# Key, query and u projections by seven products for eight, and a fixed TensorE order for the prompt attention

## The chip, the cores and the metric

The kernel runs on one core of one Trainium2 chip. The metric is the device time of one execution in microseconds. TensorE (PE) multiplies; VectorE (DVE), ScalarE (ACT) and GpSimd (POOL) do the elementwise work; SyncE (SP), ACT and POOL issue the transfers. TensorE's clock has two levels, 1.2 and 2.4 GHz; the profile gives the granted clock as a share of the upper one.

## The reference, cut to what matters

One layer of a streaming encoder for 1024 prompt tokens and 8 running streams of 16 new tokens, 1152 rows of width 1024 in all, in float32:

```python
xn = rmsnorm(x)
t = project_tokens(xn)        # gates 3x1024, u, v 512 each, fox q, k, v 512 each, mLSTM q, k, v, o, small columns
y_sg  = u * (W_s layernorm(gelu(v)) + b)          # 128-row chunks; u = gelu(.)
y_fox = softmax(q k^T / 8 + F_q - F_k, causal) v  # 8 heads x 64; prompt 1024 rows, streams with 1024 cached rows
y_ml  = mlstm(conv(q, k), v, gates)               # 4 heads x 128, chunkwise, with state
x = x + (sigmoid(g0)*(y_sg @ W0) + sigmoid(g1)*(y_fox @ W1) + sigmoid(g2)*(y_ml @ W2)) @ W_out
x = x + swiglu(rmsnorm(x)); y = rmsnorm(x)
```

Keys and values of the new rows are outputs too.

## The kernel before, in words

**Products.** Every large product is made in three passes of float32r: each operand is split in a high and a low part, and `mm3` (L113 to L120) issues high x high, high x low and low x high. A weight chunk is 1024 x 256. `load_w` (L86) loads one and splits it on ACT (L94) and DVE (L95). `proj_fm` makes a chunk feature-major, two halves of 128 columns by three groups of 384 tokens, 24 products each: six pieces, 144 products of 384 columns. `proj_tm` makes it token-major, nine tiles of 24 products of 256 columns.

**Seven products for eight.** `seven` (L513) makes a chunk by the scheme of Strassen and Winograd on halves of the contraction, the weight columns and the tokens: `combine_x` prepares the combinations of the tokens once, `weights` (L441) those of the chunk, and 7 x 2 x 12 = 168 products of 288 columns follow; DVE and ACT join the results (`plus`, L473), and SP writes them to DRAM.

**Order of the work.** The program text is a sequence of stages; a scheduler at compile time orders each engine's instructions by that sequence and by when it expects operands, and may take later work early. `keep_in_program_order` pins an instruction to its place in the text. Each engine then runs its queue in order. Stages, with their start in the trace:

1. 0 us: norm and transposition of x, the values of the attention (`v_proj`), gate scans; the first half of u (`bounce_u(0)`) and nine pieces of filler.
2. 145 us: nine chunks by `seven`: the second half of u, four of the mLSTM q and k, four gate chunks.
3. 346 us: prompt attention, head pair by head pair. Per pair the keys and queries are projected with `proj_fm` (`ev_k`, `ev_q` split them straight out of PSUM into `k1`, `k2`, `q1`, `q2`), then 8 query blocks by 2 heads follow: `scores` (L647 to L650, the causal mask as a bfloat16 product), maximum (L652), exponential (L655), scaling (L658) and `values`, which transposes the weights (L668), copies them out (L670 on DVE, L672 on ACT, half each) and multiplies with v (L683).
4. 605 us: spatial gating and the streams' attention, with cached keys and values loaded by POOL.
5. 816 us: mLSTM, four heads; each projects its v and o with `proj_tm` (`w_vo`) and runs a chain over PE, DVE, ACT and POOL. The tail of a head (`tail`: transposition L989, `ym` L993, write to DRAM) is put off until the next head's projection.
6. 1086 us: branch projections (`pz`), then output projection and feed-forward, untouched here.

**Fillers.** `fillers()` is a generator of pieces that nothing waits for at once: 18 of v and 48 of the gates (`FC` = 8 chunks). `fill(n)` puts n of them into the text: 9 ahead of stage 2, 9 after the attention, 24 in the streams' attention, 4, then 2 per head, 4 and 6 in the mLSTM, and the rest before the branch projections.

**Memory.** Pools are stacked: a stage's tiles lie where those of the closed stage before lay, and each tile waits for those it covers. The four inputs of a branch are loaded to `yl` (L1025, issued by ACT) and split to `yh`, `yl` (L438).

Of the kernel before, what the change touches and what calls it, by code (L numbers as in the profile page):

```python
# [29 lines left out]
FB = 22         # feed-forward blocks  # L30
# [10 lines left out]
def emit_(tc, A, top):  # L41
# [7 lines left out]
    mm = nc.tensor.matmul  # L49
# [22 lines left out]
    V.tensor_copy(identb, ident)  # L72
    ones = const.tile([P, P], F32, name="ones")
# [40 lines left out]
    def mm3(out, whs, wls, xhs, xls, first=True, last=True):  # L114
        """out += w^T x over the listed contraction blocks, in three passes of float32r"""
# [10 lines left out]
    def proj_fm_(w, c0, evac):  # L126
        """feature-major projection of 128 weight columns, group by group of tokens"""
# [13 lines left out]
    def proj_tm_(w, n, evac, hook=lambda t: None):  # L141
        """token-major projection of n weight columns, tile by tile of tokens"""
# [11 lines left out]
    def norm(src, gbc, tmp, parts, pin):  # L154
        """rows of a token tile: RMS norm with gain"""
# [12 lines left out]
    def flip(xg, hT, lT, ps_pool):  # L168
        """transposed, split into hT and lT"""
# [8 lines left out]
    def rms_cols(sqs, n, w, ps_pool, pin=lambda i: i):  # L178
        """1 / rms of n tokens, w to a column, from squares that are yet to be summed"""
# [10 lines left out]
    def rms_row(rs, n, w, tmp, ps_pool, pin=lambda i: i):  # L190
        """the same as a row, on every partition"""
# [13 lines left out]
    qk_d = dram("qk_d", [P, 8, T])  # L205
    g_d = dram("g_d", [3, P, KB, T])
# [4 lines left out]
    def bounce(w, c0, dst, func=AF.Copy, scale=1.0, bias=0.0):  # L211
        """feature-major projection kept in DRAM until it is needed"""
# [11 lines left out]
    def bounce_u(j):  # L224
        w = load_w(A["w_u"][j], (KB, 256))
        for i in range(2):
            yield from bounce(w, P * i, u_d[:, 2 * j + i, :], AF.Gelu)

# [8 lines left out]
    def bounce_gate(c):  # L237
        br, j = divmod(c, 4)
        w = load_w(A["w_g"][br, j], (KB, 256))
        for i in range(2):  # L240
            k = 2 * j + i
            yield from bounce(w, P * i, g_d[br, :, k, :], AF.Tanh, 0.5, bg[:, br, k:k + 1])
# [19 lines left out]
    # ================= phase A: norm of the input, transposed =================  # L262
# [38 lines left out]
    # ================= forget and input gates =================  # L301
# [21 lines left out]
    V.scalar_tensor_tensor(c, u, 1.0, e, ALU.subtract, ALU.subtract)     # (u - 1) - e  # L323
# [23 lines left out]
    # running log forget of the attention, in two exact parts, with both signs  # L347
# [15 lines left out]
    # cached rows: log forget from a key to the end of the cache  # L363
# [15 lines left out]
    # mLSTM: running sums b inside a chunk, stabiliser m, and what follows from them  # L379
# [45 lines left out]
    for _ in bounce_u(0):  # L425
        pass
    fill(9)
# [3 lines left out]
    # ================= projections that only the later phases need, in seven products for eight =================  # L431
    # Strassen and Winograd: quarters of the weights and of the tokens are combined first, the products as they leave.
# [48 lines left out]
    def combine_x(s):  # L481
# [5 lines left out]
        for n in range(0, SG, SG // 2):  # L487
# [22 lines left out]
            V.tensor_tensor(b21, b21, b11, ALU.subtract)         # t4 = b21 - t2  # L510
            keep("t4", b21)

    def seven(src, out):  # L513
# [3 lines left out]
        for a, b in (("a11", "b11"), ("a12", "b21"), ("s2", "t2"), ("s3", "t3"), ("s1", "t1"), ("s4", "b22"), ("a22", "t4")):  # L517
            for s in range(2):
# [29 lines left out]
    seven(A["w_u"][1], seven_to(lambda i: u_d[:, 2 + i], AF.Gelu))  # L548
# [8 lines left out]
    kvx = top.enter_context(ExitStack())  # L557
    kvq = pool(kvx, "kvq")
    kve = top.enter_context(ExitStack())
    kvb = pool(kve, "kvb")  # L560
    vt_ = [kvb.tile([P, NT, 256], F32, name=f"v{i}") for i in range(2)]
    for i in range(2):
        nc.scalar.dma_start(vt_[i], A["o_v"][i])

    # ================= phase B: attention over the prompt, head pair by head pair =================
# [3 lines left out]
    ps_t = pool(bs, "ps_t", 1, PSUM)  # L569
    ps_o = pool(bs, "ps_o", 1, PSUM)  # L570
    cfox = kvs.tile([P, P], BF16, name="cfox")
    G.dma_start(cfox, A["c_fox"])
    # q1 = [q_hi; q_lo], k1 = [k_hi; k_hi], q2 = [q_hi; F rows], k2 = [k_lo; F rows]; halves swapped for odd heads
# [5 lines left out]
    zr = fp.tile([P, TP], F32, tag="pe", name="zr", bufs=2)  # L579
    G.memset(zr, 0.0)  # L580
    on = fp.tile([2, TP], F32R, tag="pe", name="on", bufs=2)
# [7 lines left out]
    qbd = kvq.tile([P, 4, NB, 2 * NS], F32, name="qbd")  # L589
    G.memset(qbd, 0.0)  # L590
    kTn = kvq.tile([P, 4, P], F32, name="kTn")
    vn = kvq.tile([P, 4, P], F32, name="vn")
    wq = wk = None
    for hp in range(4):
        v_, v0 = vt_[hp // 2], P * (hp % 2)
        if hp % 2 == 0:
            wk = load_w(A["w_k"][hp // 2], (KB, 256))
            wq = load_w(A["w_q"][hp // 2], (KB, 256))

        # keys  # L600
        def ev_k(g, ps, hp=hp):
            n = min(GW, TP - g * GW)
# [9 lines left out]
            if g == 2:  # L612
                V.tensor_copy(kTn[:, hp, :], ps[:, n:GW])
# [910 lines left out]
```

## Time and profile before

| | |
|---|---|
| runs | 2123.34 us median of 3 (2115.67 to 2124.09) |
| profiled execution | span 2121.1 us from the first to the last instruction; its own time beyond that is not listed |
| mean granted TensorE clock | 0.985 |
| busy | PE 97%, PEld 93%, DVE 61%, ACT 33%, POOL 23% |
| moved | 297.96 MB, mean 140 GB/s |

Busy time of PE counts pipelined matmuls to their modelled end, so it is read together with counts: products per stretch, or the distance from one start to the next. A group line has the line, engine, operation, names, shape and count, then busy us, mean ns of one, and the idle time of the engine before them with what ended it.

### The profile page before, as it was taken

The numbers are of one execution on the slowest core, as the hardware profiler recorded it, in microseconds if no ns is written. First come the engines' busy times: TensorE is split into PE (matmuls) and PEld (weight loads), VectorE is DVE, ScalarE is ACT, GpSimd is POOL, SyncE is SP. The second block draws the span as 40 slices with busy tenths as digits, with TensorE's granted clock in tenths as the row PEclk, the third lists the DMA queues.
The fourth block names the chain that finished last, engine by engine and source line by source line (L and its number), as shares of the span: only waits on it lengthen the run. The fifth ranks groups of instructions, "written<-read, shape, count | busy, mean of one in ns | idle before, by whom it ended". The sixth has DMA issues, their size and how long they took to land. (4 is left out here: it accounts for less than half of the span.)

```text
span 2121.1 us, 37538 instructions
## 1 busy us (share of the span) xinstructions
PE 2053.6 (97%) x15448; PEld 1965.9 (93%) x15448; DVE 1292.6 (61%) x2210; ACT 707.4 (33%) x1353; POOL 485.9 (23%) x526
## 2 busy tenths in 40 slices
PE   7989999999999999999999999899999999999998
PEld 7989999888888899888999999899999999999998
DVE  5785554766533345663334656887787777855566
ACT  5232233544532223443231233332222222333342
POOL 1130002000012221011002224524554544121143
PEclk9999999999999999899999999999999999999999
DMA  4312324010148874322265534124534444455563
GB/s 164 120 51 97 115 85 162 18 59 19 63 161 298 292 239 125 123 97 72 89 199 177 182 137 149 63 100 143 171 136 163 155 157 141 154 206 205 177 223 134
DMA packets 124779, 297.96 MB, mean 140 GB/s; under 512 B 23128, under 2 KB 67352, under 8 KB 116536
## 3 DMA queue, kind: packets, MB, share of 16 engines
q1 hardware_dynamic: 62768, 164.99, 22.2%
q0 software_dynamic: 24512, 87.07, 11.7%
q10 hardware_dynamic: 37328, 43.51, 6.8%
q8 instruction: 121, 1.98, 0.4%
q14 instruction: 50, 0.41, 0.1%
HBM read 213.14 MB, written 82.55 MB: 139 GB/s over the span
## 5 line engine op out<-in xcount | busy, mean ns | idle before, releaser
L118 PE MATMUL ps_st<-xch,whi 128*128 128x288 f32 x1232 | 364.2, 296 | 5.3 <-DVE c L473 5.3
L119 PE MATMUL ps_st<-xcl,whi 128*128 128x288 f32 x1232 | 365.5, 297 | 1.8 <-DVE xcl L438 1.8
L120 PE MATMUL ps_st<-xch,wlo 128*128 128x288 f32 x1232 | 364.4, 296 | 0.9 <-POOL wlo L438 0.9
L118 PEld LDWEIGHTS ps_st<-xch,whi 128*128 128x128 f32 x1232 | 232.9, 189 | 6.6 <-DVE c L473 6.5
L119 PEld LDWEIGHTS ps_st<-xcl,whi 128*128 128x128 f32 x1232 | 232.8, 189 | 2.1 <-DVE xcl L438 2.0
L120 PEld LDWEIGHTS ps_st<-xch,wlo 128*128 128x128 f32 x1232 | 232.6, 189 | 1.1 <-POOL wlo L438 1.1
L118 PE MATMUL ps_fm<-xh,w_hi 128*128 128x384 f32 x624 | 218.6, 350 | 7.3 <-ACT bt L232 4.2
L120 PE MATMUL ps_fm<-xh,w_lo 128*128 128x384 f32 x624 | 215.9, 346 | 0.0
L119 PE MATMUL ps_fm<-xl,w_hi 128*128 128x384 f32 x624 | 215.7, 346 | 0.0
L438 ACT ACTIVATE whi<-w_raw 128x512 fp32r<-128x512 f32 x186 | 107.5, 623 | 312.0 <-DVE w_raw L458 110.1
L118 PE MATMUL po_f<-hh,w 128*128 128x288 f32 x616 | 183.2, 297 | 0.0
L118 PE MATMUL ps_tm<-w_hi,xh 128*128 128x256 f32 (+1 forms) x576 | 171.2, 297 | 11.1 <-ACT bt L232 7.1
L119 PE MATMUL po_f<-hl,w 128*128 128x288 f32 x616 | 181.7, 295 | 0.0
L120 PE MATMUL po_f<-hh,w 128*128 128x288 f32 x616 | 181.3, 294 | 0.4 <-DVE w L438 0.4
L120 PE MATMUL ps_tm<-w_hi,xl 128*128 128x256 f32 (+1 forms) x576 | 170.7, 296 | 0.1
L119 PE MATMUL ps_tm<-w_lo,xh 128*128 128x256 f32 (+1 forms) x576 | 169.9, 295 | 0.0
L438 DVE TENSOR_TENSOR wlo<-w_raw,whi 128x512 fp32r<-128x512 f32 x180 | 160.8, 922 | 5.1 <-ACT whi L438 3.0
L473 DVE TENSOR_TENSOR c<-ps_st,c 128x288 f32<-128x288 f32 x308 | 130.0, 446 | 14.9 <-PE ps_st L120 13.5
L118 PEld LDWEIGHTS ps_fm<-xh,w_hi 128*128 128x128 f32 x624 | 119.1, 191 | 13.4 <-issue 4.5
L118 PEld LDWEIGHTS ps_tm<-w_hi,xh 128*128 128x128 f32 x576 | 114.6, 199 | 14.3 <-ACT bt L232 7.9
L120 PEld LDWEIGHTS ps_fm<-xh,w_lo 128*128 128x128 f32 x624 | 119.0, 191 | 2.7 <-issue 2.4
L119 PEld LDWEIGHTS ps_fm<-xl,w_hi 128*128 128x128 f32 x624 | 119.2, 191 | 1.7 <-issue 1.2
(424 smaller groups left out, 5078.8 us busy)
## 6 DMA issues: line engine op xcount, KB each, us to landing
w_raw<-w_f SPq DMA_DIRECT2D x22, 1024.0 KB
h_d<-hq POOLq DMA_DIRECT2D x66, 288.0 KB, 2.7
kt<-ck POOLq DMA_DIRECT2D x32, 512.0 KB, 6.7
vt<-cv POOLq DMA_DIRECT2D x32, 512.0 KB, 7.0
hl<-h_d SPq DMA_DIRECT2D x28, 576.0 KB
gt<-g_d ACTq DMA_DIRECT2D x96, 144.0 KB
w_raw<-w_g SPq DMA_DIRECT2D x12, 1024.0 KB
g_d<-bt SPq DMA_DIRECT2D x48, 192.0 KB
```

What stands on the lines that cost most here:

```text
L118: mm(out, lhsT=whs[i], rhs=xhs[i], start=(first and i == 0), stop=False)
L119: mm(out, lhsT=whs[i], rhs=xls[i], start=False, stop=False)
L120: mm(out, lhsT=wls[i], rhs=xhs[i], start=False, stop=(last and i == n - 1))
L438: return act(hi, src, AF.Copy), (eng or V).tensor_tensor(lo, src, f32(hi), ALU.subtract)
L473: V.tensor_tensor(out, ps, other, ALU.add)
```

## The change

- Both chunks each of the keys, queries and u, and one gate chunk more, are made by `seven`. Keys go to the output `o_k`, queries to a new DRAM array `q_d`. Stage 2 has 15 chunks instead of 9.
- Both chunks of v (18 tiles) are made at the end of stage 1, where the first half of u and nine pieces stood. The fillers are only gate pieces, 7 chunks of 6; the first two chunks are written raw, and their tanh is applied when they are read in the branch projections.
- The attention loads a pair's keys, queries and values from DRAM (`head_load`, a pair ahead), splits them in `head_split` on ACT, DVE and POOL, and is issued as 32 steps (pair, query block) in which every TensorE instruction is pinned: scores of one head, values of the block before the last, transposition of the last block's first head, scores of the other head, transposition of the second. Twelve filler pieces stand at fixed places around the change of pairs. The mask is a float32r product; a third of the copies of the transposed weights is on DVE, the rest on ACT.
- The streams' q, k and v are loaded from DRAM at the start of their stage.

```diff
-FC = 8          # gate chunks that fill other phases; the other four go in seven products
+FC = 7
+RC = 2
...
+    def mm(*a, **k):
+        r = nc.tensor.matmul(*a, **k)
+        return tc.keep_in_program_order(r) if pinned[0] else r
...
     def fillers():
-        for j in range(2):
-            yield from bounce_v(j)
+        ws = [gate_w(0)]
         for c in range(FC):
-            yield from bounce_gate(c)
+            if c + 1 < FC:
+                ws.append(gate_w(c + 1))
...
+                if c < RC:
+                    yield from bounce(ws[c], P * i, g_d[br, :, k, :])
+                else:
+                    yield from bounce(ws[c], P * i, g_d[br, :, k, :], AF.Tanh, 0.5, bg[:, br, k:k + 1])
...
     v_proj(1)
-    for _ in bounce_u(0):
-        pass
-    fill(9)
+    for j in range(2):
+        for _ in bounce_v(j):
+            pass
...
-    seven(A["w_u"][1], seven_to(lambda i: u_d[:, 2 + i], AF.Gelu))
+    for j in range(2):
+        seven(A["w_k"][j], seven_to(lambda i, j=j: A["o_k"][2 * j + i]))
+        seven(A["w_q"][j], seven_to(lambda i, j=j: q_d[2 * j + i]))
+    for j in range(2):
+        seven(A["w_u"][j], seven_to(lambda i, j=j: u_d[:, 2 * j + i], AF.Gelu))
...
+    def head_load(hp):
+        raw = []
         for i in range(2):
+            for src in (A["o_k"], q_d):
+                r = fp.tile([P, TP], F32, tag="kq", name="kq", bufs=4)
+                for a in H:
+                    nc.sync.dma_start(r[a], src[hp, H[i], :TP])
+                raw.append(r)
...
+    def head_split(hp, raw):
+        for i in range(2):
+            kk, qq = raw[2 * i:2 * i + 2]
+            a, b = H[i], H[1 - i]
+            act(k1[i], kk, AF.Copy)
+            act(q1[i], qq, AF.Copy, scale=0.125)
+            V.tensor_tensor(k2[i][a, :], kk[a, :], f32(k1[i][a, :]), ALU.subtract)
+            G.tensor_copy(q2[i][a, :], f32(q1[i][a, :]))
+            V.scalar_tensor_tensor(q1[i][b, :], qq[b, :], 0.125, f32(q1[i][b, :]), ALU.mult, ALU.subtract)
...
-                    mm(ps[:, d:n], lhsT=identb, rhs=cfox, start=False, stop=True)
+                mm(ps[:, d:w], lhsT=identr, rhs=cfox, start=False, stop=True)
...
-                if (qi + i) % 2:
+            evacs[0] += 1
+            if evacs[0] % 3 == 0:
                     V.tensor_copy(pt_s[:, j:j + w, :], pt[:, :w, :])
...
+    pinned[0] = True
+    fill(2)
+    for n, st_ in enumerate(steps):
+        hp, qi = st_
+        if qi == 0:
+            if n:
+                values(steps[n - 2])
+                turned(steps[n - 1], 0)
+                fill(1)
+                turned(steps[n - 1], 1)
+                fill(1)
+            scores(st_, 0)
+            scores(st_, 1)
+        else:
+            scores(st_, 0)
+            if qi > 1 or n > 1:
+                values(steps[n - 2]) if n > 1 else None
+            turned(steps[n - 1], 0)
+            scores(st_, 1)
+            if qi == 1:
+                fill(1)
+            turned(steps[n - 1], 1)
+        if qi == 0 and hp < 3:
+            raw, vs[hp + 1] = head_load(hp + 1)
+        if qi == KB - 1 and hp < 3:
+            head_split(hp + 1, raw)
+    values(steps[-2])
+    for i in range(2):
+        turned(steps[-1], i)
+    values(steps[-1])
+    pinned[0] = False
-    fill(9)
...
+                if 4 * br + j // 2 < RC:
+                    act(gt, gt, AF.Tanh, scale=0.5, bias=bg[:, br, j:j + 1])
```

## Rows read from the trace of the kernel before

**Rows 1.** The page, part 1: busy us of each engine (share of the span) xinstructions.
```profile
PE 2053.6 (97%) x15448; PEld 1965.9 (93%) x15448; DVE 1292.6 (61%) x2210; ACT 707.4 (33%) x1353; POOL 485.9 (23%) x526
```
**Rows 2.** Windows of four stretches: length, busy (xcount) of PE, PEld, DVE, ACT, POOL, clock, DMA.
```profile
145.10:345.90 200.80, 200.80 (x1514) 200.80 (x1513) 111.61 (x217) 56.44 (x98) 5.80 (x3) 1.00 0.28 102
...
604.90:632.60 27.70, 23.55 (x149) 21.54 (x148) 6.49 (x9) 4.79 (x8) 6.81 (x13) 0.88 0.79 265
...
841.60:905.40 63.80, 58.49 (x390) 54.41 (x389) 44.20 (x73) 26.15 (x68) 6.97 (x6) 0.87 0.33 104
905.40:957.70 52.30, 49.43 (x374) 45.90 (x373) 31.39 (x59) 22.18 (x65) 6.86 (x5) 1.00 0.30 97
```
**Rows 3.** Windows, PE, tile ps_fm (feature-major pieces) alone: length, busy (xproducts).
```profile
345.90:373.70 27.80, 25.24 (x144) 1.00 0.49 185
...
373.70:604.90 231.20, 89.00 (x434) 1.00 0.11 38
...
604.90:815.70 210.80, 133.04 (x672) 0.97 0.77 264
...
1012.20:1085.70 73.50, 64.52 (x336) 1.00 0.33 112
```
**Rows 4.** The same for tile ps_tm (token-major tiles).
```profile
373.70:604.90 231.20, 18.90 (x113) 1.00 0.11 38
...
815.70:841.60 25.90, 25.90 (x216) 1.00 0.42 120
```
**Rows 5.** Groups by line of PE, 373.7 to 604.9 us: the attention.
```profile
L683 PE MATMUL po<-pT,v 128*64 128x128 f32 x576 | 53.0, 281 | 0.0
...
L668 PE MATMUL pt_p<-ident,pe 128*128 128x128 f32 x288 | 49.7, 281 | 0.9 <-DVE pe L658 0.9
```
**Rows 6.** Timeline of PE in the second head pair: start us, us, instruction, xcount merged.
```profile
464.17 0.60 PE L668 MATMUL pt_p<-ident,pe 128*128 128x128 f32 x4
464.53 0.48 PE L647 MATMUL ps_s<-k,q 128*128 128x512 f32 x1
464.84 0.39 PE L648 MATMUL ps_s<-k,q 128*128 128x512 f32 x1
465.07 0.39 PE L647 MATMUL ps_s<-k,q 128*128 128x512 f32 x1
...
465.85 1.52 PE L683 MATMUL po<-pT,v 128*64 128x128 f32 x22
467.31 0.66 PE L668 MATMUL pt_p<-ident,pe 128*128 128x128 f32 x4
```
**Rows 7.** Groups by line of DVE, all forms together, 373.7 to 604.9 us.
```profile
L652 DVE TENSOR_REDUCE mx<-ps_s 128x1 f32<-128x128 f32 (+7 forms) x64 | 47.8, 751 | 19.1 <-PE ps_s L650 18.7
L658 DVE TENSOR_SCALAR pe<-pe,rc 128x128 f32<-128x128 f32 (+7 forms) x64 | 33.0, 518 | 2.3
L670 DVE COPY pT<-pt_p 128x512 f32<-128x512 f32 (+3 forms) x48 | 26.5, 553 | 13.4 <-PE pt_p L668 13.2
```
**Rows 8.** Timeline of POOL where the attention's tiles are set up.
```profile
348.31 1.04 POOL L585 CAST q<-zr 64x1024 fp32r<-64x1024 f32 x1 [4.49 <-DMA g_d<-c]
...
353.47 1.03 POOL L586 CAST k<-zr 64x1024 fp32r<-64x1024 f32 x1
```
**Rows 9.** Timeline, last mLSTM head to the branch projections: PE's last pn products.
```profile
1029.64 0.65 PE L952 MATMUL pn<-Cs,qx 128*32 128x129 f32 x16
```
**Rows 10.** The same stretch, POOL: the reciprocal root of the head's norm.
```profile
1041.84 1.82 POOL L83 TENSOR_TENSOR r<-r,mhalf 128x9 f32<-128x9 f32 x1
```
**Rows 11.** The same stretch, DVE: the last scaling before the head's transposition.
```profile
1043.70 1.36 DVE L982 TENSOR_TENSOR nd<-nd,r 128x1152 f32<-128x1152 f32 x1 [3.79 <-POOL r L83]
```
**Rows 12.** The same stretch, ACT (ACTq: a transfer that ACT issues).
```profile
1054.61 0.37 ACT L993 ACTIVATE ym<-pt_h,mlg 128x128 f32<-128x128 f32 x1 [0.68 <-DMA yml_d<-ym]
...
1065.20 0.33 ACTq L1025 DMA_DIRECT2D yl<-ysg_d  x1
...
1071.00 1.17 ACT L438 ACTIVATE yh<-yl 128x1152 fp32r<-128x1152 f32 x1 [1.09 <-DMA yl<-ysg_d]
```

More of the change, by code (lines that the diff above doesn't have):

```diff
@@ L72, in emit_ @@
     V.tensor_copy(identb, ident)
+    identr = const.tile([P, P], F32R, name="identr")
+    V.tensor_copy(identr, ident)
     ones = const.tile([P, P], F32, name="ones")
@@ L205, in emit_ @@
     qk_d = dram("qk_d", [P, 8, T])
+    q_d = dram("q_d", [4, P, T])
     g_d = dram("g_d", [3, P, KB, T])
@@ L222, in emit_ @@
     V.tensor_scalar(bg, bg, 0.5, None, ALU.mult)
[L224 to L227, printed above, removed]
     def bounce_v(j):
@@ L555, in emit_ @@
     es.close()
[L557 to L563, printed above, removed]
     bs = top.enter_context(ExitStack())
@@ L568, in emit_ @@
     ps_s = pool(bs, "ps_s", 2, PSUM)
-    ps_t = pool(bs, "ps_t", 1, PSUM)
+    ps_f = pool(bs, "ps_f", 1, PSUM)
     ps_o = pool(bs, "ps_o", 1, PSUM)
-    cfox = kvs.tile([P, P], BF16, name="cfox")
-    G.dma_start(cfox, A["c_fox"])
+    banks[:] = [(ps_f, "f", 1)]
+    cfox = fp.tile([P, P], F32R, name="cfox")
+    cf = fp.tile([P, TP], F32, tag="pe", name="cf", bufs=3)
+    nc.scalar.dma_start(cf[:, :P], A["c_fox"])
+    V.tensor_copy(cfox, cf[:, :P])
     H = (slice(0, 64), slice(64, 128))
@@ L578, in emit_ @@
     k2 = [fp.tile([P, TP], F32R, name=f"k2{i}") for i in range(2)]
-    zr = fp.tile([P, TP], F32, tag="pe", name="zr", bufs=2)
+    zr = fp.tile([P, TP], F32, tag="pe", name="zr", bufs=3)
     G.memset(zr, 0.0)
-    on = fp.tile([2, TP], F32R, tag="pe", name="on", bufs=2)
+    on = fp.tile([2, TP], F32R, tag="pe", name="on", bufs=3)
     G.tensor_scalar(on, zr[:2, :], 1.0, None, ALU.add)
@@ L696, in emit_ @@
-    fill(9)
+    def head_load(hp):
+        raw = []
+        for i in range(2):
+            for src in (A["o_k"], q_d):
[3 more added lines that the diff above has]
+                raw.append(r)
+        v_ = fp.tile([P, KB, P], F32, tag="vh", name="vh", bufs=2)
+        nc.scalar.dma_start(v_, A["o_v"][hp // 2][:, :KB, P * (hp % 2):P * (hp % 2) + P])
+        return raw, v_
@@ new lines, in emit_, with scores @@
+    pes, pTs, pos, vs = {}, {}, {}, {}
+    evacs = [0]
+    def scores(n, i):
+        hp, qi = n
+        w = P * (qi + 1)
+        qs = slice(P * qi, P * qi + P)
+        ps = ps_s.tile([P, TP], F32, tag="s", name="ps_s")
+        for c in range(0, w, 512):
+            e = min(c + 512, max(w, c + 256))
+            d = w - P if w - P < e else None
+            mm(ps[:, c:e], lhsT=q1[i][:, qs], rhs=k1[i][:, c:e], start=True, stop=False)
+            mm(ps[:, c:e], lhsT=q2[i][:, qs], rhs=k2[i][:, c:e], start=False, stop=(d is None))
+            if d is not None:
+                mm(ps[:, d:w], lhsT=identr, rhs=cfox, start=False, stop=True)
+        mx = small.tile([P, 1], F32, tag="mx", name="mx")
+        V.tensor_reduce(mx, ps[:, :w], AX.X, ALU.max, negate=True)
+        pe = fp.tile([P, TP], F32, tag="pe", name="pe", bufs=3)
+        sm_ = small.tile([P, 1], F32, tag="sm_", name="sm_")
+        act(pe[:, :w], ps[:, :w], AF.Exp, bias=mx, accum_out=sm_)
+        rc = small.tile([P, 1], F32, tag="rc", name="rc")
+        V.reciprocal(rc, sm_)
+        V.tensor_scalar(pe[:, :w], pe[:, :w], rc, None, ALU.mult)
+        pes[n, i] = pe
@@ new lines, in turned @@
+    def turned(n, i):
+        pe = pes.pop((n, i))
+        pT = fp.tile([P, KB, P], F32, tag=f"pT{i}", name="pT", bufs=1)
+        for j in range(0, n[1] + 1, 4):
+            w = min(4, n[1] + 1 - j)
+            pt = ps_mm.tile([P, 4, P], F32, tag="mm", name="pt_p", bufs=2)
+            for x_ in range(w):
+                flipped(pt[:, x_, :], pe[:, (j + x_) * P:(j + x_ + 1) * P], ident)
+            evacs[0] += 1
+            if evacs[0] % 3 == 0:
+                V.tensor_copy(pT[:, j:j + w, :], pt[:, :w, :])
+            else:
+                act(pT[:, j:j + w, :], pt[:, :w, :], AF.Copy)
+        pTs[n, i] = pT
@@ new lines, in values @@
+    def values(n):
+        hp, qi = n
+        qg, qo = divmod(qi, 4)
+        if qo == 0:
+            pos[0] = ps_o.tile([P, 512], F32, tag="o", name="po")
+        po = pos[0]
+        o = slice(P * qo, P * qo + P)
+        for j in range(qi + 1):
+            for x_ in range(2):
+                mm(po[H[x_], o], lhsT=vs[hp][:, j, 64 * x_:64 * x_ + 64], rhs=pTs[n, x_][:, j, :],
+                   start=(j == 0), stop=(j == qi))
+        if qo == 3:
+            yf = fp.tile([P, 512], F32, tag="yf", name="yf", bufs=1)
+            act(yf, po, AF.Copy)
+            nc.sync.dma_start(yfox_d[:, hp, 512 * qg:512 * qg + 512], yf)
@@ new lines, in emit_ @@
+    steps = [(hp, qi) for hp in range(4) for qi in range(KB)]
+    raw, vs[0] = head_load(0)
+    head_split(0, raw)
+    pinned[0] = True
[11 more added lines that the diff above has]
+            scores(st_, 1)
+        else:
+            scores(st_, 0)
[10 more added lines that the diff above has]
+            head_split(hp + 1, raw)
@@ L697, in emit_ @@
+    values(steps[-2])
+    for i in range(2):
+        turned(steps[-1], i)
+    values(steps[-1])
+    pinned[0] = False
     bs.close()
-    kve.close()
+    banks[:] = [(ps_mm, "mm", 2)]
     ds = top.enter_context(ExitStack())
     sp = pool(ds, "smp")
+    kTn = sp.tile([P, 4, P], F32, name="kTn")
+    nc.scalar.dma_start(kTn, A["o_k"][:, :, TP:].rearrange("h p t -> p h t"))
+    vn = sp.tile([P, 4, P], F32, name="vn")
+    for i in range(2):
+        nc.scalar.dma_start(vn[:, 2 * i:2 * i + 2, :], A["o_v"][i][:, 8, :].rearrange("p (h d) -> p h d", d=P))
@@ L703, in emit_ @@
+    qbd = sp.tile([P, 4, NB, 2 * NS], F32, name="qbd")
+    G.memset(qbd, 0.0)
+    qs_ = sp.tile([P, 4, NB, NS], F32, tag="v", name="qs_", bufs=2)
+    nc.scalar.dma_start(qs_, q_d[:, :, TP:].rearrange("h p (b q) -> p h b q", q=NS))
+    for hp in range(4):
+        for i in range(2):
+            act(qbd[H[i], hp, :, NS * i:NS * i + NS], qs_[H[i], hp], AF.Copy, scale=0.125)
     ps_s = pool(ds, "ps_s3", 1, PSUM)
@@ L838, in emit_ @@
     banks.pop()
-    kvx.close()
     fill(4)
```

109 lines of the change are left out of this document (10 added, 99 removed).

## The prediction

> **What bounds the kernel now.** I read the page's first part, then windows by stage, then groups and the timeline inside the stages that change. The first part says TensorE: 97% busy, the next engine at 61% [rows 1]. That share is of modelled ends, so I go by paces. In the seven-product stage 1514 products pass in 200.8 us, 0.133 us each at full clock, and nothing waits [rows 2]; the feature-major pieces of 384 columns run at 25.24 / 144 = 0.175 us, the token-major ones of 256 columns at 25.9 / 216 = 0.120 us [rows 3, 4]. Nearly all of the span is such dense work. So time changes in two ways only: TensorE's work gets smaller, or a place opens where its queue has nothing to do. The reader should look in the rows for how much of the cover behind slow chains consists of filler, since the change spends it elsewhere.
>
> **The change part by part.**
>
> *Seven products for eight.* A full chunk is 144 products, 25.2 us; by seven it is 168 x 0.133 = 22.3 us. Six chunks change over (four of keys and queries, one of u, one gate): 6 x 2.9 = 17.5 us less. DVE, which joins the results, is busy 111.6 of 200.8 us there [rows 2], so it stays hidden at the same density; with no cover a chunk would cost DVE's 12 us. In stage 1 nine token-major tiles (25.9 us) replace six pieces of u (25.2): +0.7.
>
> *The attention's own work.* From 345.9 to 604.9 us are 259.0 us. Out of them go 576 products of keys and queries (100.8 us) and 113 of v (13.6) [rows 3, 4]: 144.6 us are left, 36.2 per head pair. What must be in a pair: by the code 24 score products of 512 columns, 16 of 256 and 8 of 384, at 0.23 (464.84 to 465.07), 0.12 and 0.175: 8.8 us; 288 / 4 = 72 transpositions at 0.36 for four: 6.5; 576 / 4 = 144 value products at 1.46 for 22: 9.6 [rows 5, 6]. That is 24.9. The other 11.3 us are changes between kinds of product (the first score product behind transpositions takes 0.31 instead of 0.23 [rows 6]), table loads and waits.
>
> After the change a step has five groups, hence five changes. The values' own is in their pace; four at 0.08 for eight steps are 2.6 us. The 16 mask products become float32r of 128 columns, which no row shows; between nothing and the 0.23 of a 512-column one I take the 0.12 of 256 columns: 1.9. The pinned order makes every product wait behind the one ahead of it: a transposition that waits for DVE's scaling holds the next scores, and with them the next maximum. DVE's work per pair is (47.8 + 33.0 + 2/3 of 26.5) / 4 = 24.6 us [rows 7] and an estimated 2.5 of reciprocals, 27, against TensorE's 29.4. So near a balance queues will not mesh fully; I take 2.5 us of waits (0 to 7, where 7 is what remains of the 11.3). A pair: 31.9.
>
> At the start the tiles that hold the F rows wait until the last results of the seven-product stage are written: POOL begins at 348.3, and its four casts end at 354.5 [rows 8]. POOL's copies of q and SP's row transfers come behind them, an estimated 5 us, so scores start at about 359.5; the two pinned filler pieces (8.4 us) end at 354.3. A hole of 5 us. At the end the last block's chain has nothing beside it: 3 us. Sum 4 x 31.9 + 5 + 3 = 135.6 against 144.6: 9 us less (19 less with no waits, 16 more with 7 us of waits and masks at 0.23). At a change of pair the new split (some 5 us each on ACT and DVE, 2 on POOL) and its SP transfers lie behind two filler pieces, two transpositions and a group of values, about 11 us; uncovered it would be 3 us a pair.
>
> The Trainium skill, *TensorEngine Tiling (Array Packing)*, Key Properties, says that a change of tiling mode drains the engine. Values use half the columns (128*64), so each of their groups would drain twice; the trace holds it in the 1.46 us for 22 of them, the change included, and cannot part it from the products. By that rule fewer and longer groups alone bring the 19 us of the case without waits, the second rival below.
>
> *Streams' attention.* Behind the attention now lie 103 leftover products of v, 12.4 us, while the first keys are loaded; even so that stretch has 23.6 of 27.7 us busy at clock 0.88 [rows 2, 4]. They go; 30 filler pieces remain where 672 / 24 = 28 are used now [rows 3], so some move forward: +4 us (0 to 12). The new loads of q, k, v and eight ACT copies are issued beside the cached keys' transfers.
>
> *mLSTM.* Of 42 pieces 12 go into the attention and 28 into the streams: 2 are left for four heads, against 20 now. Moving them costs nothing; the holes they leave do. Inside a head the next head's v and o tiles can move up, but their gate tile has one buffer, so only four tiles (11.5 us) fit before the head's norm is done. What a head costs when the chain shows: the first takes 63.8 us at clock 0.87, the second 52.3 at 1.00, with 390 and 374 products [rows 2]. Two heads lose 8.4 us of filler each; between 0 and 11.5 each I take 5: +10.
>
> The last head has no next one. Now 336 filler products, 58.8 us, lie from its start to the branch projections [rows 3]. Its last pn products end at 1030.3 [rows 9]; POOL's root ends at 1043.7 [rows 10], the scaling at 1045.1 [rows 11]. Of these 14.8 us TensorE has 3 of its own: a hole of 12. Before that, in the 18 us from the head's first product, another 4. Then `ym` is copied and written by about 1057; the branch inputs lie where this head's tiles were, and the third one's load takes 5.8 us to its split [rows 12]; with the earlier start I take 8. Together +24 (10 if the inputs' space is free early, 35 if all loads queue behind the tail).
>
> The Trainium skill, *TensorE: Matmul & The Clock Gate*, HAM oscillation, warns that gaps between bursts of matmuls bring the clock back to 1.2 GHz. The 0.87 above, a mean of the two levels, agrees. By it the branch products behind the hole would start at half rate, an estimated 3 us on top.
>
> The tanh of two gate chunks on ACT, 16 operations, lies beside branch products; ACT is the idler engine there.
>
> *Sum.* -17.5 + 0.7 - 9 + 4 + 10 + 24 = +12. The profiled span is 2121.1 us; the median of the runs is 2.2 above. Forecast 2121.1 + 12 + 2.2 = 2135 us, 0.6% slower.
>
> **Rivals.**
>
> *The holes don't open* (faster). The scheduler moves the next head's tiles and the branch products up into the last heads. For it: the first branch needs nothing of this head. Against: its inputs' place in memory. Of 34 us of holes some 6 remain: 2107. It decides from the point where they stay under 11 us, since all other terms add up to -22.
>
> *The pinned order runs free of waits.* TensorE's 29.4 exceeds DVE's 27; against it, the chain of maximum, exponential and scaling has one step to finish. 10 us less: 2125.
>
> *DVE sets the attention's pace.* In the wide blocks its work is about TensorE's, and a pinned queue cannot step aside. +25: 2160.
>
> **How the numbers follow.** Forecast 0.45 (own range 2120 to 2152), holes stay shut 0.27, no waits 0.18, DVE 0.10. A measurement of this kernel tells 0.5%, 11 us, from no change. Faster: 0.25 of the first rival, 0.04 of the second, 0.29. The same: 0.02, 0.14 and 0.08 of the forecast's low end, 0.24. Slower: 0.37 and 0.10, 0.47. The range goes from below the first rival to beyond the third: 2095 to 2166.
>
> **What would show it.** Seven products: 15 chunks at 22.3 us, 2520 products without a gap. Attention: 186 us with 288 filler products in it; TensorE's waits name DVE's scaling or ACT's copies. mLSTM: no feature-major product behind the first head, and waits of the transposition of the last head and of the first branch products of some 20 us, with a clock under 1. It is wrong if the branch products start within 8 us of the last head's pn products, or if the attention needs more than 200 us.

## The result and the profile after

The changed kernel takes 2184.94 us (median, 2174.86 to 2188.74) against 2123.72 for the kernel before on the same chip: ratio 1.0296, 95% interval 1.0264 to 1.0329, slower. The profiled execution spans 2179.3 us against 2121.1. The forecast was 2135: its direction came true, its size is 50 us short and its range (2095 to 2166) does not hold the result. First the engines' shares on the page, which answer to [rows 1]:

```profile
PE 2040.0 (94%) x15592; PEld 1966.2 (90%) x15592; DVE 1322.9 (61%) x2252; ACT 715.1 (33%) x1377; POOL 496.7 (23%) x533
```

TensorE is busy 13.6 us less and the span is 58.2 longer. The windows by stage say where. Their columns are those of [rows 2]; in order: seven products, start of the attention, the rest of it, streams, the four mLSTM heads, the branch products.

```profile
149.00:483.80 334.80, 334.80 (x2522) 334.80 (x2521) 188.50 (x367) 90.60 (x160) 4.78 (x3) 1.00 0.28 101
483.80:506.50 22.70, 8.79 (x50) 8.15 (x48) 5.43 (x5) 5.67 (x6) 4.31 (x4) 0.78 0.87 245
506.50:686.50 180.00, 167.57 (x1360) 146.81 (x1360) 124.74 (x241) 104.28 (x226) 14.26 (x11) 0.97 0.27 77
686.50:914.20 227.70, 214.87 (x1973) 189.84 (x1971) 84.68 (x140) 54.42 (x103) 52.51 (x98) 0.99 0.75 254
914.20:955.30 41.10, 35.59 (x254) 32.68 (x253) 31.01 (x56) 14.19 (x23) 9.35 (x4) 0.96 0.39 119
955.30:1003.50 48.20, 41.49 (x318) 39.86 (x318) 33.52 (x55) 21.82 (x63) 7.58 (x6) 0.89 0.27 76
1003.50:1065.90 62.40, 53.24 (x351) 47.54 (x350) 31.13 (x67) 16.01 (x60) 2.10 (x2) 0.81 0.18 65
1065.90:1132.20 66.30, 39.81 (x246) 34.11 (x245) 23.26 (x46) 23.71 (x82) 4.15 (x4) 0.73 0.30 97
1132.20:1292.90 160.70, 158.14 (x1152) 155.93 (x1153) 88.71 (x175) 40.90 (x65) 28.25 (x32) 0.97 0.55 168
```

The clock column is the quickest guide: 1.00 in the seven products, 0.78 in the start of the attention, then a fall from head to head, 0.96, 0.89, 0.81, 0.73. A stage's length alone misleads, because filler was moved between stages. So the table takes each stage without it (a feature-major product at 0.175 us, a token-major one at 0.120), and from each head also its other products at the pace that they have in the last head of the kernel before, where the clock is 1.00 and nothing waits:

| step of the forecast | forecast, us | measured, us |
|---|---|---|
| six chunks by seven products | -17.5 | -17.3 (334.8 / 15 = 22.32 a chunk; six of them less 864 x 0.175) |
| stage 1 | +0.7 | +3 (TensorE waits 8.4 for the gelu copies of v, 6.4 before) |
| attention's own work | -9 | +8 (202.7 - 50.4 = 152.3 against 144.6) |
| streams | +4 | +3 |
| mLSTM heads 1 to 3 | +10 | +13 (-7, +6, +14) |
| last head, start of the branch products | +24 | +44 (36 and 8) |
| the rest | 0 | +4 |
| sum | +12 | +58 |

Where the heads' time goes is seen in TensorE's waits from 914 to 1140 us (what it waited for, us in total, times, longest):

```profile
PE pt_h L1021 <- DVE nd L1014: 10.2, 1, 10.2
PE ps_tm L53 <- ACT to L937: 8.3, 3, 4.7
PE ps_st L53 <- DVE wt L965: 7.6, 5, 3.0
PE pu L53 <- DVE Cc L974: 6.2, 5, 3.8
PE pz L53 <- ACT yh L450: 6.2, 2, 5.6
```

These are links of the heads' own chain, which filler covered before. In all TensorE is idle for 47.9 us in the four heads, 8.8 before. The last head in the timeline (start, duration, engine, instruction), answering to [rows 9 to 12]:

```profile
1107.00 0.65 PE L53 MATMUL pn<-Cs,qx 128*32 128x129 f32 x16
...
1119.05 1.83 POOL L95 TENSOR_TENSOR r<-r,mhalf 128x9 f32<-128x9 f32 x1
1120.91 1.36 DVE L1014 TENSOR_TENSOR nd<-nd,r 128x1152 f32<-128x1152 f32 x1 [5.13 <-POOL r L95]
1122.33 1.12 PE L1021 MATMUL pt_h<-ident,nd 128*128 128x128 f32 x4 [10.22 <-DVE nd L1014]
...
1126.63 0.33 ACTq L1057 DMA_DIRECT2D yl<-ysg_d  x1
1131.26 0.33 ACTq L1057 DMA_DIRECT2D yl<-ysg_d  x1
1132.20 1.33 PE L53 MATMUL pz<-yh,w_hi 128*128 128x288 f32 x4 [5.61 <-ACT yh L450]
1134.00 0.44 PE L53 MATMUL pz<-yh,w_lo 128*128 128x288 f32 x1
1134.24 0.44 PE L53 MATMUL pz<-yl,w_hi 128*128 128x288 f32 x1
```

From the last pn product to the transposition TensorE has almost nothing to do; the branch inputs are asked for only behind the last copy, at 1126.6; and the first branch products follow at 0.24 us, not at 0.133: the lower clock level. The same trace holds one thing more. The inputs of the second branch, which have other space, are asked for between 1087.0 and 1104.8 and are split by 1112.6, 20 us before the first branch product; but TensorE's queue has the first branch next. Whether the second branch, taken first, would fill this hole was not tried.

### The profile page after: what moved, and what is told of

Its sections match the earlier page's. It is cut to its first block, busy times and chain, and to the rows that moved or that the text cites. A ratio compares the mean times of both kernels' runs of the same rounds, so it can differ in the third digit from the quotient of the medians.

```text
span 2179.3 us, 38038 instructions
## 1 busy us (share of the span) xinstructions
PE 2040.0 (94%) x15592; PEld 1966.2 (90%) x15592; DVE 1322.9 (61%) x2252; ACT 715.1 (33%) x1377; POOL 496.7 (23%) x533
## 3 DMA queue, kind: packets, MB, share of 16 engines
q1 hardware_dynamic: 65328, 175.74, 23.4%
## 5 line engine op out<-in xcount | busy, mean ns | idle before, releaser
L450 ACT ACTIVATE whi<-w_raw 128x512 fp32r<-128x512 f32 x222 | 128.6, 623 | 398.6 <-PE ps_x L53 173.2
L53 PE MATMUL po_f<-hh,w 128*128 128x288 f32 x1232 | 248.6, 296 | 0.7 <-DVE w L450 0.7
L53 PEld LDWEIGHTS po_f<-hh,w 128*128 128x128 f32 x1232 | 198.2, 188 | 1.3 <-DVE w L450 1.1
L450 DVE TENSOR_TENSOR wlo<-w_raw,whi 128x512 fp32r<-128x512 f32 x216 | 174.5, 839 | 11.0 <-ACT whi L450 7.4
L485 DVE TENSOR_TENSOR c<-ps_x,c 128x288 f32<-128x288 f32 x210 | 92.8, 454 | 129.2 <-PE ps_x L53 110.7
L53 PE MATMUL pz<-yh,w_hi 128*128 128x288 f32 x384 | 113.0, 300 | 7.4 <-ACT yh L450 7.2
L53 PE MATMUL ps_fm<-xh,w_hi 128*128 128x384 f32 x336 | 118.8, 353 | 0.6 <-ACT bt L228 0.6
L53 PEld LDWEIGHTS ps_tm<-w_hi,xl 128*128 128x128 f32 x576 | 116.2, 202 | 1.1 <-issue 0.4
L53 PEld LDWEIGHTS ps_tm<-w_lo,xh 128*128 128x128 f32 x576 | 116.1, 202 | 0.6
L53 PE MATMUL ps_fm<-xh,w_lo 128*128 128x384 f32 x336 | 115.8, 345 | 0.0
```

The lines of the kernel that those rows point to most:

```text
L53: r = nc.tensor.matmul(*a, **k)
L485: V.tensor_tensor(out, ps, other, ALU.add)
```

## The experiments

Medians are of the runs of each kernel; ratios against the kernel before, with 95% intervals.

**Is it the filler?** Ten gate chunks as filler in the changed kernel (the weights of the later ones are loaded when they start):

```diff
-FC = 7
+FC = 10
...
```

> The changed kernel with ten gate chunks as filler instead of seven (two by seven products instead of five), so that 20 pieces are left for the four mLSTM heads and the tail instead of 2. Theory A (what the heads and the tail lost was their filler, and with it the clock): three chunks cost 3 x 2.9 = 8.7 us more on TensorE, and the 57.6 us lost between the first mLSTM product and the end of the branch projections come back almost whole: 2185 + 9 - 58 = 2136, with 244 us from the first score product of the mLSTM to the first branch product as before, and a granted clock of at least 0.95 there instead of 0.83. Rival B (the holes come from the head's own chain and its loads, the filler only shifts them): the 18 pieces add up to their own 75 us less what fits in 48 us of idle time, so 2185 + 9 + 0 to 27, about 2195 to 2220.

Measured 2129.63 us, ratio 1.0030 (1.0014 to 1.0046). The third and fourth head and the branch products:

```profile
...
965.00:1016.60 51.60, 50.95 (x382) 46.54 (x381) 20.10 (x45) 16.40 (x60) 6.65 (x3) 1.00 0.21 74
1016.60:1090.10 73.50, 73.50 (x455) 69.41 (x454) 27.02 (x46) 23.91 (x52) 2.08 (x2) 1.00 0.34 112
1090.10:1242.70 152.60, 152.60 (x1153) 152.60 (x1152) 89.42 (x176) 44.41 (x68) 27.12 (x32) 1.00 0.61 190
```

The last head with 336 filler products is 7.2 us longer than the one without any (66.3, which holds 120 token-major products instead), and nothing waits in it. Three chunks made as filler cost TensorE 3 x 2.88 = 8.6 us more than by seven products, so in all 2179.3 + 8.6 - 2127.2 = 60.7 us of span came back. The reverse, in the kernel before:

```diff
-FC = 8
+FC = 5
```

> The kernel before with five gate chunks as filler instead of eight (seven by seven products instead of four): nothing of the change but its lack of filler, 2 pieces for the mLSTM and the tail instead of 20. Theory A: three chunks by seven products save 8.7 us, and the heads and the tail lose the 57.6 us that they lost in the changed kernel: 2124 - 9 + 58 = 2173, with the transposition of the last head waiting some 10 us and a clock near 0.83. Rival B (the loss needs the rest of the change, such as keys and queries in DRAM or the new loads): 2124 - 9 + 0 to 15, that is 2115 to 2130. The forecast's own price of the holes (34) would give 2149.

Measured 2174.90, ratio 1.0237 (1.0213 to 1.0262). Last head and branch products:

```profile
1061.00:1127.60 66.60, 39.83 (x247) 34.15 (x246) 23.30 (x46) 23.66 (x81) 4.15 (x4) 0.73 0.29 96
1127.60:1288.50 160.90, 159.36 (x1153) 157.05 (x1154) 88.51 (x175) 33.84 (x49) 27.22 (x32) 0.96 0.55 168
```

The same 66 and 161 us, without anything else of the change. Its span is 2173.2, and 2121.1 - 8.6 + 60.7 = 2173.2. Taken away, the pieces give the loss; put back, they end it. This settles what the main loss is: 18 pieces of filler, 76 us of products that the change took out or spent earlier, covered 61 us of waits and slow products.

**Which pieces?** The 18 are parted: 12 pieces, all for the last head and the tail; or 6, two for each of the last three heads. Both edits are shown against the kernel with ten chunks:

```diff
-FC = 10
+FC = 9
-        fill(2)
+        fill(2 if h == 0 else 0)
```

> The changed kernel with nine gate chunks as filler: 12 pieces more, all of them for the last mLSTM head and what follows it, while the three heads between get none (2 pieces in the first, as in the changed kernel). It parts the price of the holes. Reading of the changed kernel's trace: 24.3 us of idle time and 8 us of low clock from the last head on, and 8.1 us in the branch products, 40 us; that is 2185 + 2 x 2.9 - 40 = 2151. By the forecast's own sizes (24 for the tail, 10 for the heads): 2185 + 6 - 24 = 2167. If the holes between the heads weigh as much as the rest (29 each): 2162.

Measured 2147.30, ratio 1.0115 (1.0081 to 1.0150).

```diff
-FC = 10
+FC = 8
```

> The counterpart: eight gate chunks as filler, 6 pieces more, two for each of the second to fourth heads, and none behind the last head. By the reading of the trace (some 18 us lost between the heads, of them 7 to 13 as idle time and the rest as clock): 2185 + 2.9 - 18 = 2170. By the forecast's 10 us: 2178. Together with the kernel for the tail alone the two gains should add up to the 57.6 us that ten chunks brought back; if they add up to more, each closes part of the same hole; if to less, a hole needs both.

Measured 2146.22, ratio 1.0109 (1.0076 to 1.0142). In spans the tail's pieces brought 2179.3 + 5.8 - 2143.7 = 41 us, the heads' 2179.3 + 2.9 - 2143.9 = 38, together 80, where both at once brought 61. So some 19 us are closed by either, and my 18 for the heads was less than half. The third and fourth head of the second kernel, and its branch products, show how:

```profile
...
1006.90:1058.50 51.60, 50.95 (x383) 46.55 (x382) 20.09 (x45) 16.39 (x60) 6.65 (x3) 1.00 0.18 63
1058.50:1100.30 41.80, 24.56 (x167) 20.21 (x165) 20.79 (x44) 13.71 (x40) 2.08 (x2) 0.77 0.42 135
1100.30:1260.70 160.40, 159.13 (x1153) 156.81 (x1154) 91.42 (x177) 43.14 (x67) 28.24 (x32) 0.96 0.56 172
```

The third head, with 48 filler products more, takes 51.6 us instead of 62.4, its clock 1.00 instead of 0.81. And the last head's token-major tiles (120 products of them lie in the last head of the changed kernel) are done a head earlier. The four heads hold 98, 338, 218 and 2 token-major products here and 98, 217, 218 and 121 in the changed kernel (216 make a head's nine tiles; a count may include two of a neighbour's): with two pieces a head all nine tiles of the next head are made a head ahead, without them only four, and five are left for the head itself. Why the pieces make that difference no run shows.

**Is the low clock a price of its own?** Six pieces in the last head and behind it whose results nobody reads:

```diff
...
+        if h == 3:
+            for _ in range(2):
+                idle_piece()
...
-    fill(4)
+    for _ in range(4):
+        idle_piece()
```

> The changed kernel with 6 pieces of 24 products more in the last mLSTM head and behind it, of the size of a filler piece (25 us of products), whose results nobody reads. They take no work from anywhere else, so whatever they gain is not the filling of the hole but what the hole does to the products around it. In the changed kernel the last head takes 66.3 us with 26.5 us of idle time and the products between them at half rate (granted clock 0.73), and the branch products 160.7 us instead of 152.6. Theory (the low clock is a price of its own, some 12 us in the last head and 8 in the branch products): the pieces cost nothing where TensorE is idle, the rest of the last head runs faster, and the branch products take 152.6: 2185 - 8 - 0 to 8 = 2169 to 2177. Rival (only idle time counts): the pieces that do not fit push the chain back, 2185 to 2195. The forecast named 3 us for the clock: 2182.

Measured 2189.17, ratio 1.0315 (1.0276 to 1.0353): the rival's number. Windows of the last head, the branch products, the chain from the first pu to the last pn product, and the first 104 branch products:

```profile
1071.20:1143.60 72.40, 58.30 (x391) 53.51 (x390) 21.31 (x44) 21.53 (x80) 4.16 (x4) 0.90 0.22 73
1143.60:1305.80 162.20, 157.64 (x1152) 155.44 (x1153) 91.23 (x177) 42.96 (x67) 28.33 (x32) 0.98 0.56 174
1094.00:1107.70 13.70, 13.70 (x103) 12.29 (x104) 8.35 (x22) 2.23 (x8) 0.00 (x0) 1.00 0.12 39
1143.60:1167.00 23.40, 18.84 (x105) 16.64 (x106) 11.29 (x14) 11.89 (x19) 0.00 (x0) 0.86 0.62 193
```

and the same two short stretches of the changed kernel:

```profile
1088.70:1107.40 18.70, 12.71 (x69) 9.98 (x67) 11.82 (x25) 5.50 (x11) 0.00 (x0) 0.73 0.44 140
1132.20:1154.10 21.90, 19.34 (x105) 17.13 (x106) 8.78 (x12) 10.22 (x18) 0.00 (x0) 0.78 0.52 156
```

The chain took 13.7 us at clock 1.00 instead of 18.7 at 0.73, although 37 products were put into it. At most these 5 us go with the clock, for the clock is not the only difference. In the changed kernel DVE splits three of the second branch's inputs inside the chain (busy 11.82 us against 8.35), and a step of the chain stands behind the last of these splits:

```profile
1104.46 1.36 DVE L450 TENSOR_TENSOR yl<-yl,yh 128x1152 fp32r<-128x1152 f32 x1 [0.69 <-ACT yh L450]
...
1106.14 0.49 PE L53 MATMUL pn<-va,wt 128*128 128x129 f32 x2 [1.41 <-DVE nd L987]
```

With the unread products these splits come only behind the chain, from 1135.7 on, so some 1.4 of the 5 us are theirs. The forecast's 3 us for the clock, given there beside the Trainium skill's *TensorE: Matmul & The Clock Gate*, HAM oscillation, were for another place, the branch products. The gain did not last: most of the other unread products ran as one block from 1114.9 to 1130.2 ahead of the transposition, which came 22.5 us behind the last pn product instead of 14.9. Then two loads of the second branch went out ahead of the first branch's (1130.3 and 1134.5 before 1138.2), so that the first branch products began 10.6 us behind the last transposition instead of 6.1. And they ran no faster, 104 of them in 23.4 us with clock 0.86 against 21.9 with 0.78. So the clock alone does not explain their 8 us.

**What holds the first branch products?** The four loads of their inputs, 4 us apart on ACT's queue, were the next suspect:

```diff
-            nc.scalar.dma_start(f32(lo), yd[:, k, :])
+            (nc.scalar if n else nc.sync).dma_start(f32(lo), yd[:, k, :])
```

> The changed kernel with the four loads of the first branch's inputs issued on SP's queue instead of ACT's. In the changed kernel they are issued at 1126.6, 1131.3, 1135.3 and 1139.1 us, 4 us apart, each behind ACT's splitting of the one before. Theory (this row of loads holds the first branch products): on SP they go out one behind the other within 2 us, the first 104 products take some 15 us instead of 21.9, and the time falls by 6 to 8: 2177 to 2179. Rival (the low clock holds them, 0.78 in this stretch): at most 2 us, 2183 to 2185.

Measured 2185.57, ratio 1.0297 (1.0273 to 1.0321).

```profile
1133.96 6.22 SPq L1057 DMA_DIRECT2D yl<-ysg_d  x4
1140.19 1.15 ACT L450 ACTIVATE yh<-yl 128x1152 fp32r<-128x1152 f32 x1
```

The four went out over 6 us, not within 2, and the first was ready only at 1140.2. The first branch product came 8.9 us behind the last transposition instead of 6.1, and the first 104 took 18.9 us instead of 21.9: 27.8 us from the last transposition to the 104th, before this edit 28.0, with clock 0.91 and 0.78. The edit moved the wait and did not shorten it; neither the queue nor the clock alone holds this stretch. The same edit where nine chunks are filler (below):

> The kernel with nine gate chunks as filler, a free attention order and a bf16 mask, with the same four loads on SP's queue. With nine chunks the first 104 branch products took 24.3 us instead of 13.8. By the theory of the loads most of that comes back: 2125 - 8 = 2117, level with ten chunks. By the rival: 2123 to 2125.

Measured 2125.30, ratio 1.0009 (0.9992 to 1.0027), against 2124.81 without it: no gain either. What is left is the time of the transfers (four of 576 KB, among gate tiles of 144 KB each); that was not tried.

**The start of the attention.** In the changed kernel the scores begin 22.7 us after the seven products with 8.4 us of cover. SP's queue, then the instructions that follow:

```profile
488.62 0.33 SPq L105 DMA_DIRECT2D w_raw<-w_g  x1
...
493.72 0.32 SPq L229 DMA_DIRECT2D g_d<-bt  x1
494.30 0.57 SPq L598 DMA_DIRECT2D q<-on  x1
...
496.50 2.11 SPq L608 DMA_DIRECT2D kq<-o_k  x2
501.74 1.06 ACT L618 ACTIVATE k<-kq 128x1024 fp32r<-128x1024 f32 x1 [8.04 <-DMA kq<-o_k]
505.23 1.22 DVE L622 SCALAR_TENSOR_TENSOR q<-kq,q 64x1024 fp32r<-64x1024 f32 x1 [1.19 <-ACT q L619]
506.51 0.58 PE L53 MATMUL ps_s<-k,q 128*128 128x256 f32 x1 [13.34 <-DVE q L622]
```

The first pair's loads moved ahead of the constant rows:

```diff
+    raw, vs[0] = head_load(0)
     zr = fp.tile([P, TP], F32, tag="pe", name="zr", bufs=3)
...
-    raw, vs[0] = head_load(0)
     head_split(0, raw)
```

> The changed kernel with the first head pair's loads of keys and queries issued ahead of the preparation of the constant rows (zeros, ones), which in the changed kernel stand ahead of them on SP's queue and reach 496.5 us. Theory C (the order on SP's queue makes the hole): the loads are issued about 7 us earlier, at 489, and the scores begin 7 us earlier: 2178. Rival D (the space of the loaded tiles comes free only with the last writes of the seven-product stage, and the constant rows are then late instead): no more than 2 us, 2183 to 2185.

Measured 2188.32, ratio 1.0296 (1.0270 to 1.0322); scores 22.3 us after the seven products.

```profile
489.27 1.33 SPq L597 DMA_DIRECT2D kq<-o_k  x2
493.58 0.33 SPq L229 DMA_DIRECT2D g_d<-bt  x1
494.01 1.09 SPq L597 DMA_DIRECT2D kq<-q_d  x2
498.51 1.06 ACT L607 ACTIVATE k<-kq 128x1024 fp32r<-128x1024 f32 x1 [4.96 <-DMA kq<-o_k]
```

Asked for 7 us earlier, the keys were there 3 us earlier: 9.2 us under way instead of 5.2. And the queries' load stands behind the second filler piece's write, which waits for that piece. Then the values' load out of the way as well; the next gate chunk's weights were to come later too, but their transfer was issued at 488.7 as before, so only the values tell:

```diff
...
-        nc.scalar.dma_start(v_, A["o_v"][hp // 2][:, :KB, P * (hp % 2):P * (hp % 2) + P])
+        (nc.scalar if hp else nc.sync).dma_start(v_, A["o_v"][hp // 2][:, :KB, P * (hp % 2):P * (hp % 2) + P])
...
     head_split(0, raw)
+    vs[0] = load_v(0)
```

> The kernel with the early loads of the first head pair, and besides the values' load of this pair (1 MB) issued behind them on SP's queue and the next gate chunk's weights (1 MB) loaded three pieces later. With the early loads alone the first keys were asked for 7 us earlier, but took 9 us to land instead of 5, all DMA engines being busy at 0.99 from 488 us on. Theory (the transfers' place in the traffic makes the hole): the first keys and queries land 4 to 5 us after 489.5 and the scores begin near 500 instead of 506: 2188 - 6 = 2182, against 2185 for the changed kernel 2179 to 2182. Rival (POOL's copies and the constant rows, which wait for the last writes of the stage before, come last): scores at 504 or later, 2185 to 2188.

Measured 2178.02, ratio 1.0265 (1.0226 to 1.0303). The keys came at 497.0, 7.4 us after the issue, and the scores begin 18.2 us after the seven products, at 502.1:

```profile
502.11 0.58 PE L53 MATMUL ps_s<-k,q 128*128 128x256 f32 x1 [8.87 <-DVE q L616]
```

The scores gained 4.5 of the 6 us that were expected. With the values' 1 MB off ACT's queue the keys were 7.4 us under way instead of 9.2. This fits the Trainium skill, *DMA: Bandwidth & Descriptors*, Queues, rings and completion order, by which a DMA engine takes turns between the queues that have work for it. One profile of each kernel does not show that this is the reason.

**The fixed order.**

```diff
-    pinned[0] = True
+    pinned[0] = False
```

> The changed kernel with the same attention, but its products not kept in the order of the program. By the forecast's step (a pinned queue waits where a free one steps aside, and its two filler pieces at the start end before the scores can begin) the filler pieces move forward into the hole at the start: 14 us and some clock less there, about 2168. But the pieces that move are then missing at the changes of head pair: if those need them, up to 3 us a pair return, 2168 to 2177. Rival (the fixed order itself is a gain, since the free one has more changes between kinds of product, 36.2 us a pair as before instead of 34): 2168 + 8 = 2176 or more, no better than 2185 if the pairs also lose their cover.

Measured 2171.83, ratio 1.0230 (1.0200 to 1.0261). Start and rest of the attention:

```profile
483.40:511.30 27.90, 24.90 (x138) 23.30 (x137) 5.42 (x5) 7.04 (x9) 4.88 (x4) 1.00 0.70 210
511.30:672.00 160.70, 156.17 (x1274) 129.77 (x1272) 125.21 (x241) 102.18 (x223) 12.65 (x11) 1.00 0.30 84
```

135 filler products, not 48, lie in the start, and 4 us of hole remain of 14. Without their filler (153 products) the pairs take 133.9 us, pinned 138.0. So the fixed order cost 14 us, 10 at the start and 4 in the pairs, and gained nothing.

**The mask.**

```diff
-    cfox = fp.tile([P, P], F32R, name="cfox")
+    cfox = fp.tile([P, P], BF16, name="cfox")
...
-                mm(ps[:, d:w], lhsT=identr, rhs=cfox, start=False, stop=True)
+                mm(ps[:, d:w], lhsT=identb, rhs=cfox, start=False, stop=True)
```

> The changed kernel with the mask products of the attention in bf16 again (identity and mask as bf16), as in the kernel before; nothing else. The forecast puts a float32r mask product at 0.12 us; the trace of before has 0.04 for one in bf16. 64 products x 0.08 = 5 us less: 2180. If changes between the kinds of operand cost TensorE something, the gain is gone: 2185 or a little more. The difference is near what a measurement tells; the pace in the trace decides.

Measured 2180.56, ratio 1.0270 (1.0232 to 1.0307), and the stretch from the first score to the last value product lasts 180.0 us in both:

```profile
506.10:686.10 180.00, 168.61 (x1360) 142.79 (x1360) 124.87 (x241) 103.98 (x226) 14.21 (x11) 0.97 0.25 76
```

The mask's type is worth nothing here, so the 4 us between the medians are not its doing.

**The filler moved.** No product added or taken away; four pieces at the start of the attention, none inside it:

```diff
...
-    fill(2)
+    fill(4)
...
-                fill(1)
                 turned(steps[n - 1], 1)
-                fill(1)
...
-            if qi == 1:
-                fill(1)
```

> The changed kernel with its filler moved and no product added or taken away: 4 pieces at the start of the attention instead of 2, none at its changes of head pair or behind its first steps (12 before), so that 10 pieces instead of 2 are left for the heads and the tail. Theory (the change spent its filler where little waited): the heads get back what 6 pieces brought them alone, some 40 us, the start of the attention 8, and the changes of pair lose 3 us each, four with the first: 2185 - 40 - 8 + 12 = 2149. Rival (the changes of pair need theirs: split, transfers and the one-step chain show by 8 us each, and the first steps by 4): 2185 - 48 + 40 = 2177.

Measured 2175.71, ratio 1.0261 (1.0214 to 1.0309). The sum of 2149 missed. The profile is of the fastest of four runs, 13.3 us of span below the changed kernel's. In order, the pairs, the streams and the heads:

```profile
508.60:658.70 150.10, 132.37 (x1120) 110.68 (x1120) 120.33 (x239) 96.81 (x214) 14.23 (x11) 0.92 0.25 64
658.70:899.00 240.30, 219.11 (x1972) 191.82 (x1969) 87.67 (x141) 56.25 (x107) 52.24 (x98) 0.96 0.70 245
899.00:1117.10 218.10, 191.38 (x1352) 174.78 (x1352) 118.81 (x220) 78.19 (x232) 24.37 (x16) 0.94 0.29 95
```

Two of the three terms held: the pairs without filler lost 150.1 - 138.0 = 12 us, as said, and the heads did 192 products more in the same 218 us, 34 regained of 40. The hole at the start shrank by 5 us instead of 8. And the streams, with as many filler products as before, took 12.6 us more; their transpositions waited 16.9 us for ACT's exponentials instead of 6.2. Why is open: the later chunks' weights are loaded when the chunk starts, and the pieces fall elsewhere.

**Together.** Ten chunks, free order, bf16 mask:

> What the first runs point to, in one kernel: seven products for keys, queries and u as in the change, but ten gate chunks as filler (20 pieces for the heads and the tail), the attention's order left free, and the mask in bf16. From the runs: 2130 for ten chunks, 13 less for the free order, up to 5 less for the mask: 2112 to 2117, 0.2 to 0.5% faster than before. If the free order takes its filler from the pairs at a cost that only shows when all else is closed, 2125.

Measured 2116.78, ratio 0.9969 (0.9950 to 0.9987): 0.3% under the kernel before and the best of all. That is less than the 0.5% that I took a measurement to tell, though the interval leaves out 1. With nine chunks:

```diff
-FC = 10
+FC = 9
```

> The kernel that has ten gate chunks as filler, a free attention order and the bf16 mask, with nine chunks instead of ten: 14 pieces for the heads and the tail instead of 20, 2.9 us less on TensorE. With ten chunks the last head had 336 filler products over holes of some 50 us, so it can spare some: if the tail's holes stay shut with 6 pieces, 2117 - 3 = 2114. If each piece taken away opens as much as the last ones closed (6 pieces for 41 us between the heads), it is 2130 or more.

Measured 2124.81, ratio 1.0013 (0.9990 to 1.0035). The heads with 336 filler products took 219.1 us instead of 240.1 with 480, so 144 products of 25.2 us were taken away for 21 us, and the branch products took 163.2 instead of 152.6. The result lies between the two numbers that were expected: the six pieces of the tail covered some 11 us (8 between the medians and the 2.9 that a chunk by seven saves).

## Why the prediction fell short, step by step

- *Seven products*: right, 22.32 us a chunk, 2520 products without a gap. The +0.7 of stage 1 was no term: the pieces of u are in the six chunks already, and the tiles of v only come from later stages. What the stage lost is 3 us of waits.
- *Attention*: the pace was right, the start wrong. From 551.0 to 686.5 us three pairs with 192 filler products take 135.5 - 33.6 = 101.9 us, by the forecast 3 x 31.9 + 3 = 98.7. The first one costs 36, at clock 0.88. The hole at the start is 14 us instead of 5: I counted POOL's copies and the row transfers, but put at nothing the loads of the pair's own keys and queries, and SP's queue with a filler piece's write ahead of them. 202.7 us against my own limit of 200. The step is 17 us off, 9 of them by this hole: the smaller of the two that failed.
- *Streams*: right (+3 for +4). *Mask*: in the sum it came to nothing.
- *mLSTM heads*: +13 for +10, but not as drawn: not 5 each in two heads, but a gain of 7 in the first and losses of 6 and 14 that grow to the last head's, as only four of a head's nine tiles are made ahead of it.
- *Last head*: the step that failed most, 44 us instead of 24: "Before that, in the 18 us from the head's first product, another 4". From its first product to its last pn the head takes 41.5 us for products that at full clock take 23.7: 18 over, 8 of them idle and most of the rest at the low clock (0.83 over the stretch), where it was 2 before. So +16 instead of 4. The two other terms, 12 for the norm and 8 for the branch inputs, are right: from the last pn to the first branch product 24.8 us for some 4 us of products, +20. What they left out is the 8 us that the branch products then lose while the other three inputs arrive; the prediction names 3 us for them, outside its sum. What holds these products in the end is open.
- *The sum*: 61 us behind 18 pieces of filler were priced at 34. I worked out the holes one by one, each as if the products around it kept their pace.
- *Rivals*: that the holes stay shut is refuted by the waits; that DVE sets the attention's pace too (behind the start TensorE waits once for DVE's splitting, 1.8 us, and 0.4 us for its copies). Nor does the pinned order run free of waits: behind the start they add up to 9.4 us, 2.4 a pair, for my 2.5. The free order came closest to the forecast's attention: 188.5 us against my 186.

## What to carry to other kernels

A piece of work that can run anywhere is cover, and taking it out saves its length only where nothing waits behind it: list who lives under it before pricing the saving. Prices of single holes do not add up. Here holes worked out at full pace gave 34 of 61 us, since TensorE also ran slower around them, and pieces put back in two groups gave 41 and 38, more than both together. The sure price is a run of the kernel before without the cover. Where a stage's inputs move to DRAM, its first loads belong in the sum, with their queue and the transfers beside them.

## What was not expected of the hardware

- With products between its links whose results nobody reads, a chain took 13.7 us instead of 18.7, at a granted clock of 1.00 instead of 0.73; some 1.4 us of that come from other work that left the chain, and behind it the gain was lost.
- A transfer issued 7.2 us earlier landed only 3.2 us earlier, and asking for the branch inputs from another queue did not move the 104th branch product: 27.8 against 28.0 us behind the last transposition.
- With 64 mask products of 128 columns in float32r or in bf16 the attention behind its start took the same 180.0 us.
